# mLSTM stage of a two-block layer on one core: gate rows in four column groups, stabiliser maxima by one fp32r product, denominators as a further value column

## The chip, the cores and the metric

The kernel runs on one core of a Trainium2 chip. The metric is the device time of one execution in microseconds (us); of several runs the median is given. TensorE (PE) has a separate weight loader (PEld); DVE is VectorE, ACT is ScalarE, and SP issues nearly all of the DMAs here.

## The reference, cut to what matters

Two blocks act one after the other on x of 256 tokens by 2048 features, all in float32. The first is attention and a gated feed-forward; the change doesn't touch it. The second has an mLSTM branch with 8 heads (keys of 128, values of 256):

```
proj = h @ w_in + b_in          # q, k, v, o, z_a, i_pre (8), f_pre (8), ...
b = cumsum(log_sigmoid(f_pre)); d_intra = b_l - b_s + i_pre_s   (s <= l)
m_row = max(d_inter, max_s d_intra)            # running stabiliser
scores = (q k^T) * 128**-0.5 * exp(d_intra - m_row)
num = scores @ v;  den = sum_s scores          # (plus the carried state)
h_out = num / max(|den|, exp(-m_row))
h_a = rms_norm(sigmoid(o) * h_out) * silu(z_a);  y_a = h_a @ w_proj_a
```

The kernel computes the mLSTM without chunks: with u = i_pre - b and M = running maximum of u, the weight of key s for query l is exp(-max(M_l - u_s, 0)), masked above the diagonal, and the floor of the denominator is exp(-(b + M)).

## The kernel before

All matrix products with weights go through `step`s. A step is one transfer of 128 x 2048 float32 weights (`raw`), a split into a high part `hi` on ACT (L245) and a low part `lo` on DVE (L246), both in fp32r, and 24 products of 128 x 512 on PE (`group_mm`, L321 to L323: hi by hi, lo by hi, hi by lo), twelve for each half of the tokens (`th`). There are four `raw` buffers and two of `hi` and `lo`. Activations are kept as such pairs too (`khi`, `klo`). `later(n, f)` runs f after the n-th next step; a scheduler then sets the order of each engine's instructions within the data dependences.

The part that the change touches follows the second norm (`barrier2`, where DVE and ACT compute the norm of x and PE has to wait):

- 16 steps of v: the results are evacuated to `V2` (L968), one 128 x 512 tile for each pair of heads and token half.
- One step `if` for the gates: 16 weight columns (8 of i, 8 of f) are padded to 128, loaded as 1 MB, split, and multiplied as 96 fp32r products of 128 x 128 with 128 columns (L983 to L985). `if_rows` then computes log-sigmoid, the cumulated sum b, u (L1015) and M (L1017) on 8 partitions, on ACT and DVE. Three steps later `tr` turns u and exp(-(b+M)) into columns by four small PE transposes (L1024, L1025, `rowT`).
- Then q, k, o and z_a; after every z_a group come two heads (`mlstm`), each in four stages that `later` spreads over the following steps: `qkT` transposes; scores `st` (L1079, L1080) and `mb` (L1082), a float32 product that copies row h of M to all partitions; `den` (L1100 to L1102), three products of the weights `w` with a column of ones, and `num` (L1103 to L1105), three products with v; `hT` transposes.

Of the kernel before, what the change touches and what calls it, by code (L numbers as in the profile page):

```python
# [16 lines left out]
D = 2048  # L17
# [43 lines left out]
K_M0 = 771  # L61
K_M1 = 772
K_SEL = 773
NCONST = 774


def _consts():
    c = np.zeros((128, NCONST), np.float32)
    c[:, K_ID:K_ID + 128] = np.eye(128, dtype=np.float32)
    p = np.arange(128)[:, None]  # L70
    d = 128 + p - np.arange(256)[None, :]
    cnt = ((d >= 0) & (d <= 128)).astype(np.float64)
# [12 lines left out]
    c[:, K_M1] = m1
    c[::32, K_SEL] = 1.0
    return c


def build(tc, A, out):  # L90
# [22 lines left out]
    def ktile32(name="k32"):  # L113
        return kp.tile([128, 512], F32, name=name, tag="k")
# [13 lines left out]
    cols = pp.tile([128, NCOL], F32, name="cols")  # L128
    ident = pp.tile([128, 128], F32, name="ident")
    ones = pp.tile([128, 2], F32, name="ones")  # L130
    ksm = pp.tile([128, NCONST - K_INVA], F32, name="ksm")
    epsc = pp.tile([128, 2], F32, name="epsc")
    x = pp.tile([128, 2, D], F32, name="x")
    cb = pp.tile([128, D], F32, name="cb")
    mod = pp.tile([128, 96], F32, name="mod")
# [21 lines left out]
    def xs_hl(K, k, a, th):  # L157

        e = K[k]
        if isinstance(e, dict):  # L160
            t, c = e[th][a]
            return t[:, c:c + 128]
        return e[:, a, th * 128:(th + 1) * 128]
# [162 lines left out]
        act.activation(dst, ss, AF.Sqrt, bias=epsc[:, 0:1], scale=1.0 / n)  # L326
        dve.reciprocal(dst, dst)

    onesr = pp.tile([128, 128], F32R, name="onesr")
    act.activation(onesr, ones[:, 0:1].to_broadcast([128, 128]), AF.Copy)  # L330

    def row_bcast(c16, g, grow, key):
        hl = sp.tile([128, 2, 4], F32, name="rhl", tag="rhl", bufs=2)
        hr = sp.tile([128, 4], F32R, name="rhr", tag="rhr", bufs=2)
        c = c16[:, 4 * g:4 * g + 4]
        act.activation(hr, c, AF.Copy)
        dve.tensor_copy(hl[:, 0, :], hr.bitcast(F32))
        dve.tensor_sub(hl[:, 1, :], c, hl[:, 0, :])
        d = [kp.tile([128, 512], F32R, name="dg", tag="k") for _ in range(2)]
        for i in range(4):  # L340
            for a in range(2):
                act.activation(d[a][:, i * 128:(i + 1) * 128], ident, AF.Copy, scale=hl[:, a, i:i + 1])
        r = ktile32("rowb")
        if grow is not None:
            nc.sync.dma_start(r, bcast_row(grow[:, 512 * g:512 * g + 512], 512))

        def end():
            p = at_tile("row")
            for a in range(2):
                pe.matmul(p, onesr, d[a], start=(a == 0), stop=(a == 1))  # L350
            if grow is None:
                act.activation(r, p, AF.Copy)
            else:
                dve.tensor_mul(r, r, p)
            GP[key] = r
        later(0, end)
# [6 lines left out]
    nc.sync.dma_start(ksm, A["consts"][:, K_INVA:NCONST])  # L363
# [567 lines left out]
    dn_group(NG - 1)  # L931

    H3 = {}
    mM = pp.tile([128, 128], F32, name="mM")

    def barrier2():
        assert len(gq) <= 16, len(gq)
        nc.sync.dma_start(mM, A["consts"][:, K_MM:K_MM + 128])
        barrier(H3)

    steps[-1] = steps[-1][:5] + (barrier2,)
# [22 lines left out]
                 post=post if kq == 3 else None, fill_n=int(kq in fill))  # L964

    def v2_evac(g, th, p, b):
        V2[g, th] = ktile32("v2")
        dve.tensor_add(V2[g, th], p, b)  # L968

    for g in range(4):  # L970
        tok_steps("v", g, v2_evac)

    R = {}
    uc = pp.tile([128, 32], F32, name="ucols")
# [12 lines left out]

    def if_rows(p):
        rows = []
# [7 lines left out]
        act.activation(g, p[:, :S], AF.Identity, bias=cols[:, C_IF:C_IF + 1])  # L997
# [18 lines left out]
        M = ztile("rowM")  # L1016
# [4 lines left out]
        def tr():  # L1021
# [5 lines left out]
        R["M"] = M  # L1027
        later(3, tr)

    step(A["w_if"], 2048, if_step)  # L1030

    OS = {}
    SZ = {}
# [9 lines left out]
    def za_evac(g, th, p, b):  # L1043
        z = ttile("zb")
        dve.tensor_add(z, p, b)
        SZ[g, th] = ztile("siluz")
# [13 lines left out]
    def mlstm(h, at):  # L1060
# [12 lines left out]
        def s1():  # L1073
            q, k = st["qk"][:, 0:S], st["qk"][:, S:2 * S]
            if h == 0:
                dve.tensor_scalar(hnh, col("headnorm_w_2", 0, 16), 0.5, None, op0=OP.mult)
            M = R["M"]
# [7 lines left out]
            dve.scalar_tensor_tensor(w[:, 0:128], mb[:, 0:128], uc[:, h:h + 1], mM, op0=OP.subtract, op1=OP.max)  # L1085
            dve.tensor_scalar(w[:, 128:256], mb[:, 128:256], uc[:, h:h + 1], 0.0, op0=OP.subtract, op1=OP.max)
            dve.scalar_tensor_tensor(w[:, 256:384], mb[:, 128:256], uc[:, 8 + h:9 + h], mM,
                                     op0=OP.subtract, op1=OP.max)
            act.activation(w, w, AF.Exp, scale=-1.0)
            dve.scalar_tensor_tensor(w, sc[:, 0:384], 128.0 ** -0.5, w, op0=OP.mult, op1=OP.mult)  # L1090
            st["w"] = w

        def s2():
            w = st["w"]
            g, c0 = h // 2, (h % 2) * 256
            v0 = V2[g, 0][:, c0:c0 + 256]
            v1 = V2[g, 1][:, c0:c0 + 256]
            num = at_tile("num")
            dn = at_tile("den")
# [12 lines left out]
            t = ktile32("hn")  # L1112
            jk = ktile32("jk")
            for i in range(2):
                dve.scalar_tensor_tensor(t[:, i * 256:(i + 1) * 256], num[:, i * 256:(i + 1) * 256],
                                         da[:, i:i + 1], OS[g, i][:, c0:c0 + 256], op0=OP.mult, op1=OP.mult)
                act.activation(jk[:, i * 256:(i + 1) * 256], t[:, i * 256:(i + 1) * 256], AF.Square,
                               accum_out=ss[:, i:i + 1])
# [224 lines left out]
def _layout(inp):  # L1343
# [50 lines left out]
    wif = np.zeros((D, 128), np.float32)  # L1394
    wif[:, 0:8] = w[:, 8192:8200]
    wif[:, 32:40] = w[:, 8200:8208]
    a["w_if"] = _blocks(wif)[0]
# [22 lines left out]
```

## Time and profile before

| | |
|---|---|
| three runs | 2477.57, 2478.49, 2479.67 us; median 2478.49 |
| profiled execution | 2476.79 us, of which its span is 2475.0 |
| busy | PE 2410.0 us (97%), weight loads 2023.7 (82%), DVE 1584.8 (64%), ACT 1151.2 (47%) |
| DMA | 597 MB, 241 GB/s on the mean |
| mean granted TensorE clock | 0.991 of full speed |

The span runs from the first to the last instruction; 1.8 us of the execution lie around it. Busy shares are means over stages with different limits, so they say only where to look.

### The profile page before, as it was taken

The page shows a single profiled execution, that of the slowest core. Times are in us where ns is not written, and L with a number is a line of the kernel's source. Part 1 is how long each engine was busy: PE and PEld are TensorE (multiplying, and loading weights), DVE is VectorE, ACT ScalarE, POOL GpSimd, SP SyncE. Part 2 cuts the span into 40 slices and gives each one's busy share as a digit, 9 for nine tenths or more (in the row PEclk, how much of TensorE's full clock was granted, in tenths as well). Part 3 has the DMA queues.
Part 4 walks back from the last instruction along what each step waited for, and adds up shares of the span by engine and source line. Part 5 has one row for each costly group of instructions (what it writes and reads, how often), then busy time and mean ns, then how long its engine had stood idle before and what let it go on. Part 6 is the DMA issues. An engine that isn't in the chain of part 4 may idle for free.

```text
span 2475.0 us, 30384 instructions
## 1 busy us (share of the span) xinstructions
PE 2410.0 (97%) x12508; PEld 2023.7 (82%) x12508; DVE 1584.8 (64%) x1727; ACT 1151.2 (47%) x1415; POOL 0.2 (0%) x4
## 2 busy tenths in 40 slices
PE   6999989999999999999899999999999999999998
PEld 4888988878888888888778888888888888888887
DVE  5888888876666566666664556565456666554555
ACT  5433887653443433334553335455333443444344
POOL 0000000000000000000000000000000000000000
PEclk9999999999999999999999999999999999999999
DMA  8987879847777677677635554555557667555553
GB/s 319 339 332 276 312 280 356 335 187 278 287 266 283 252 282 290 240 298 285 217 115 205 184 191 177 188 178 191 187 211 250 242 249 251 201 198 209 189 193 132
DMA packets 90436, 597.36 MB, mean 241 GB/s; under 512 B 10165, under 2 KB 10805, under 8 KB 20665
## 3 DMA queue, kind: packets, MB, share of 16 engines
q1 hardware_dynamic: 90296, 595.41, 66.1%
q8 instruction: 98, 1.61, 0.3%
q14 instruction: 42, 0.34, 0.0%
HBM read 593.28 MB, written 2.10 MB: 241 GB/s over the span
## 4 chain that ended last, share of the span: by engine, by line
PE 89%; DVE 4%; ACT 3%; DMA 3%; issue 1%; SPq 0%; ACTq 0%; DVEq 0%
PE gu L322 6%; PE gu L321 6%; PE gu L323 6%; PE dn L322 3%; PE dn L323 3%; PE dn L321 3%; PE wo L322 2%; PE wo L321 2%; PE wo L323 2%; PE v L321 2%; PE v L322 2%; PE v L323 2%; DVE lo L246 2%; DMA graw<-i_ada_k 2%; PE z_a L321 1%; PE ga L321 1%
## 5 line engine op out<-in xcount | busy, mean ns | idle before, releaser
L246 DVE TENSOR_TENSOR lo<-raw,hi 128x2048 fp32r<-128x2048 f32 (+3 forms) x446 | 917.1, 2061 | 715.2 <-ACT hi L245 714.9
L245 ACT ACTIVATE hi<-raw 128x2048 fp32r<-128x2048 f32 (+3 forms) x446 | 769.1, 1730 | 1037.2 <-PE gu L323 251.3
L321 PE MATMUL gu<-hi,khi 128*128 128x512 f32 x688 | 268.3, 390 | 0.0
L322 PE MATMUL gu<-lo,khi 128*128 128x512 f32 x688 | 267.8, 389 | 0.0
L323 PE MATMUL gu<-hi,klo 128*128 128x512 f32 x688 | 267.7, 389 | 0.0
L172 DVE SCALAR_TENSOR_TENSOR graw<-graw,cb 128x2048 f32<-128x2048 f32 x112 | 255.9, 2285 | 11.1 <-DMA graw<-i_w_ada 8.7
L322 PEld LDWEIGHTS gu<-lo,khi 128*128 128x128 f32 x688 | 129.2, 188 | 26.8 <-DVE lo L246 0.2
L323 PEld LDWEIGHTS gu<-hi,klo 128*128 128x128 f32 x688 | 129.2, 188 | 26.7
L321 PEld LDWEIGHTS gu<-hi,khi 128*128 128x128 f32 x688 | 129.1, 188 | 26.5
L322 PE MATMUL dn<-lo,khi 128*128 128x512 f32 x336 | 131.0, 390 | 1.5 <-DVE lo L246 1.5
L323 PE MATMUL dn<-hi,klo 128*128 128x512 f32 x336 | 130.8, 389 | 0.0
L321 PE MATMUL dn<-hi,khi 128*128 128x512 f32 x336 | 130.5, 390 | 0.0
L285 PE MATMUL qk<-h,lo 128*128 128x256 f32 x256 | 74.7, 292 | 3.1 <-DVE lo L246 3.1
L283 PE MATMUL qk<-h,hi 128*128 128x256 f32 x256 | 75.7, 296 | 0.1
L322 PEld LDWEIGHTS dn<-lo,khi 128*128 128x128 f32 x336 | 63.1, 188 | 15.2 <-DVE lo L246 2.4
L284 PE MATMUL qk<-h,hi 128*128 128x256 f32 x256 | 74.3, 290 | 0.0
L509 PE MATMUL e<-h,lo 128*128 128x256 f32 x256 | 72.8, 287 | 1.6 <-DVE lo L246 1.6
L323 PEld LDWEIGHTS dn<-hi,klo 128*128 128x128 f32 x336 | 63.1, 188 | 13.2
L321 PEld LDWEIGHTS dn<-hi,khi 128*128 128x128 f32 x336 | 63.1, 188 | 13.1
L507 PE MATMUL e<-h,hi 128*128 128x256 f32 x256 | 73.7, 289 | 0.0
L508 PE MATMUL e<-h,hi 128*128 128x256 f32 x256 | 72.9, 286 | 0.0
L285 PEld LDWEIGHTS qk<-h,lo 128*128 128x128 f32 x256 | 51.0, 199 | 3.5 <-DVE lo L246 3.5
(439 smaller groups left out, 4987.1 us busy)
## 6 DMA issues: line engine op xcount, KB each, us to landing
raw<-i_w_gu SPq DMA_DIRECT2D x88, 1024.0 KB, 4.8
graw<-i_ada_t SPq DMA_DIRECT2D x64, 1024.0 KB, 5.9
graw<-i_w_ada SPq DMA_DIRECT2D x48, 1024.0 KB, 4.8
raw<-i_w_dn SPq DMA_DIRECT2D x44, 1024.0 KB, 4.8
graw<-i_ada_k SPq DMA_DIRECT2D x32, 1024.0 KB, 7.0
raw<-i_w_out SPq DMA_DIRECT2D x32, 1024.0 KB, 5.7
raw<-i_w_s SPq DMA_DIRECT2D x24, 1024.0 KB, 6.8
raw<-i_w_qk SPq DMA_DIRECT2D x16, 1024.0 KB, 7.3
```

The source lines that it names most:

```text
L172: dve.scalar_tensor_tensor(g, g, 1.0, cb, op0=OP.mult, op1=OP.mult, accum_out=dst)
L245: act.activation(hi[:, b:e], r[:, b:e], AF.Copy)
L246: dve.tensor_sub(lo[:, b:e], r[:, b:e], hi[:, b:e].bitcast(F32))
L283: pe.matmul(dst, wh, K[k][:, 0, :], start=s, stop=False)
L284: pe.matmul(dst, wh, K[k][:, 1, :], start=False, stop=False)
L285: pe.matmul(dst, wl, K[k][:, 0, :], start=False, stop=e)
L321: pe.matmul(dsts[th], xh, wh, start=s, stop=False)
L322: pe.matmul(dsts[th], xh, wl, start=False, stop=False)
L323: pe.matmul(dsts[th], xl, wh, start=False, stop=e)
L507: pe.matmul(dst, hv[:, i, c0:c0 + 128], H[k][:, 0, :], start=(k == k0), stop=False)
L508: pe.matmul(dst, hv[:, i, c0:c0 + 128], H[k][:, 1, :], start=False, stop=False)
L509: pe.matmul(dst, lv[:, i, c0:c0 + 128], H[k][:, 0, :], start=False, stop=(k == k1 - 1))
```

## The change

- **Gate rows.** `w_if` is no longer a step. Its 16 columns come as one 128 x 256 tile (`wif`, float32, not split). 64 float32 products have 16 weight columns as the stationary operand and 128 tokens of `khi` or `klo` as the moving one; product k goes to partitions 32*(k mod 4) of the result, so that four accumulations lie in four column groups of the array. ACT copies the four 16-row parts into one tile (`parts`, zeroed on DVE), and two steps later one float32 product with a 0/1 matrix (`ifq`) adds them into the rows that `if_rows` expects.
- **Maxima.** M is split once into an fp32r pair on partitions 0 to 7 and 32 to 39 of `mhl`; `mb` is one fp32r product of 64 rows with a 0/1 selector instead of a float32 product of 8 rows.
- **Denominators.** Each head's values get a 257th column of ones (`V2` tiles of 2 x 272, set by a memset), so `num` yields the denominator too, and the three `den` products go. `num` takes two banks where it took one beside `den`.
- **Buffers.** `V2` moves to the pool `zp`, `siluz` to `kp`, `rowM` to `tp`. The mask `mM` and the selector are loaded at `barrier2` instead of at the start. Small tiles are padded: `x`, `cb`, `mod` move from byte 18432, 34816, 43008 to addresses 64 higher; the pools of large tiles start at multiples of 128 before and after.

```diff
+K_MSEL = 774
+K_IF = 782
+    for h in range(8):
+        c[[h, 32 + h], K_MSEL + h] = 1.0
+    for p in range(128):
+        i = p % 16
+        c[p, K_IF + (i if i < 8 else 24 + i)] = 1.0
...
-    ksm = pp.tile([128, NCONST - K_INVA], F32, name="ksm")
-    epsc = pp.tile([128, 2], F32, name="epsc")
+    ksm = pp.tile([128, K_IF - K_INVA], F32, name="ksm")
+    epsc = pp.tile([128, 16], F32, name="epsc")
...
-                pe.matmul(p, onesr, d[a], start=(a == 0), stop=(a == 1))
+                pe.matmul(p, oner[:, 0:1].to_broadcast([128, 128]), d[a], start=(a == 0), stop=(a == 1))
...
     def barrier2():
-        nc.sync.dma_start(mM, A["consts"][:, K_MM:K_MM + 128])
+        t = ztile("mlc")
+        mlc["hl"] = rtile("mhl")[0:64, 0:S]
+        mlc["M"], mlc["sel"] = t[:, S:S + 128], t[:, S + 128:S + 192]
+        nc.sync.dma_start(mlc["M"], A["consts"][:, K_MM:K_MM + 128])
+        nc.sync.dma_start(mlc["sel"], A["consts"][:, K_IF:K_IF + 64])
+        act.activation(msel, ksm[0:64, K_MSEL - K_INVA:K_MSEL - K_INVA + 8], AF.Copy)
         barrier(H3)
...
     def v2_evac(g, th, p, b):
-        V2[g, th] = ktile32("v2")
-        dve.tensor_add(V2[g, th], p, b)
+        t = zp.tile([128, 2, 272], F32, name="v2", tag="z")
+        dve.memset(t[:, :, 256:257], 1.0)
+        dve.tensor_add(t[:, :, 0:256], p.rearrange("p (a c) -> p a c", a=2), b.rearrange("p (a c) -> p a c", a=2))
+        V2[g, th] = t
...
-    def if_step(hi, lo):
+    def if_load():
+        R["wif"] = ktile32("wif")[:, 0:256]
+        nc.sync.dma_start(R["wif"], A["w_if"])
+    def if_post():
+        wt = R["wif"]
         p = acc_tile("if")
         for th in range(2):
-            dst = p[:, th * 128:(th + 1) * 128]
-            for k in range(KT):
-                wh, wl = hi[:, 128 * k:128 * k + 128], lo[:, 128 * k:128 * k + 128]
-                xh, xl = xs_hl(H3, k, 0, th), xs_hl(H3, k, 1, th)
-                pe.matmul(dst, wh, xh, start=(k == 0), stop=False)
-                pe.matmul(dst, wh, xl, start=False, stop=False)
-                pe.matmul(dst, wl, xh, start=False, stop=(k == KT - 1))
-        if_rows(p)
+            for i in range(4):
+                for a in range(2):
+                    for j in range(4):
+                        k = 4 * i + j
+                        pe.matmul(p[32 * j:32 * j + 16, th * 128:(th + 1) * 128], wt[:, 16 * k:16 * k + 16],
+                                  xs_hl(H3, k, a, th).bitcast(F32), start=(i == 0 and a == 0),
+                                  stop=(i == 3 and a == 1))
+        parts = ttile("ifp")[:, 0:S]
+        dve.memset(parts, 0.0)
+        for j in range(4):
+            act.activation(parts[32 * j:32 * j + 16, :], p[32 * j:32 * j + 16, 0:S], AF.Copy)
+        def end():
+            q = acc_tile("ifq")
+            pe.matmul(q[0:64, 0:S], mlc["sel"], parts, start=True, stop=True)
+            if_rows(q)
+        later(2, end)
...
-    step(A["w_if"], 2048, if_step)
+        hl = mlc["hl"]
+        act.activation(hl, ones[0:64, 0:1].to_broadcast([64, S]), AF.Copy, scale=0.0)
+        act.activation(hl[0:8, :], M[0:8, 0:S], AF.Copy)
+        dve.tensor_sub(hl[32:40, :], M[0:8, 0:S], hl[0:8, :].bitcast(F32))
+    for g in range(4):
+        tok_steps("v", g, v2_evac, post=(None, None, if_load, if_post)[g])
...
-            pe.matmul(mb[:, 0:S], ident[0:8, h:h + 1].to_broadcast([8, 128]), M[0:8, 0:S], start=True,
-                      stop=True)
+            pe.matmul(mb[:, 0:S], msel[:, h:h + 1].to_broadcast([64, 128]), mlc["hl"], start=True, stop=True)
...
-            pe.matmul(dn[:, 0:1], w[:, 0:128], ones[:, 0:1], start=True, stop=True)
-            pe.matmul(dn[:, 1:2], w[:, 128:256], ones[:, 0:1], start=True, stop=False)
-            pe.matmul(dn[:, 1:2], w[:, 256:384], ones[:, 0:1], start=False, stop=True)
-            pe.matmul(num[:, 0:256], w[:, 0:128], v0, start=True, stop=True)
-            pe.matmul(num[:, 256:512], w[:, 128:256], v0, start=True, stop=False)
-            pe.matmul(num[:, 256:512], w[:, 256:384], v1, start=False, stop=True)
+            num = [at_tile("num") for _ in range(2)]
+            pe.matmul(num[0][:, 0:257], w[:, 0:128], v0, start=True, stop=True)
+            pe.matmul(num[1][:, 0:257], w[:, 128:256], v0, start=True, stop=False)
+            pe.matmul(num[1][:, 0:257], w[:, 256:384], v1, start=False, stop=True)
...
-            act.activation(da[:, 0:2], dn[:, 0:2], AF.Abs)
+            for i in range(2):
+                act.activation(da[:, i:i + 1], num[i][:, 256:257], AF.Abs)
```

On PE, where the v steps end and q begins, 96 products stood between them, of which these are the last, with q behind them:

```order
L985 MATMUL if<-khi,lo 128x128
L983 MATMUL if<-khi,hi 128x128
L984 MATMUL if<-klo,hi 128x128
L985 MATMUL if<-khi,lo 128x128
L321 MATMUL q_11026<-hi,khi 128x512
L322 MATMUL q_11026<-lo,khi 128x512
```

Now there are 16 rows of four products, of which these are the last, and `ifq` follows behind the second step of q, with 77 products from there to the first `rowT`:

```order
L1001 MATMUL if<-khi,wif 16x128 x4
L1001 MATMUL if<-klo,wif 16x128 x4
L328 MATMUL q_10981<-hi,khi 128x512
...
L330 MATMUL q_10982<-hi,klo 128x512
L1011 MATMUL ifq<-ifp,mlc 64x256
L328 MATMUL q_10981<-hi,khi 128x512
...
L329 MATMUL k_11141<-lo,khi 128x512
L1051 MATMUL rowT<-ident,rowB 128x8
L330 MATMUL k_11141<-hi,klo 128x512
```

So the gates' products shrink, `ifq` is new, and `rowT` moved from the q steps into the second step of k.

On PE, in head 0, `den` and `num` stood between two steps of o:

```order
L323 MATMUL o_11555<-hi,klo 128x512
L1100 MATMUL den<-ones,w 128x1
L1101 MATMUL den<-ones,w 128x1
L1102 MATMUL den<-ones,w 128x1
L1103 MATMUL num<-v_10502,w 128x256
L1104 MATMUL num<-v_10502,w 128x256
L1105 MATMUL num<-v_10504,w 128x256
L321 MATMUL o_11554<-hi,khi 128x512
```

The same place now:

```order
L330 MATMUL o_11542<-hi,klo 128x512
L1129 MATMUL num<-v_10506,w 128x257
L1130 MATMUL num<-v_10506,w 128x257
L1131 MATMUL num<-v_10509,w 128x257
L328 MATMUL o_11541<-hi,khi 128x512
```

Three products went, and each of the others has one column more. `mb` keeps its place behind `st`.

On DVE, the gate rows' chain (`rowE`, `rowQ`, `rowB`) had its six polynomial steps in one piece, and the evacuations of q (`tq`) stood behind it; now they stand in it:

```order
L1006 TENSOR_SCALAR rowQ<-rowQ 8x256
L246 TENSOR_TENSOR lo<-raw,hi 128x2048
L1008 SCALAR_TENSOR_TENSOR rowQ<-rowQ 8x256 x6
L1009 SCALAR_TENSOR_TENSOR rowQ<-rowQ,rowE 8x256
L1011 SCALAR_TENSOR_TENSOR rowQ<-rowQ,rowE 8x256
L246 TENSOR_TENSOR lo<-raw,hi 128x2048
```

The same stretch of the chain now:

```order
L253 TENSOR_TENSOR lo<-raw,hi 128x2048
L1035 SCALAR_TENSOR_TENSOR rowQ<-rowQ 8x256
L1087 TENSOR_TENSOR tq<-q_10981,bq 128x512
L1035 SCALAR_TENSOR_TENSOR rowQ<-rowQ 8x256
L1087 TENSOR_TENSOR tq<-q_10982,bq 128x512
L1035 SCALAR_TENSOR_TENSOR rowQ<-rowQ 8x256 x3
L253 TENSOR_TENSOR lo<-raw,hi 128x2048
L1035 SCALAR_TENSOR_TENSOR rowQ<-rowQ 8x256
```

The two passes of `lo` stay in the chain, and two evacuations joined it.

## Rows read from the trace of the kernel before

**Rows 1.** The page, part 4: shares of the chain that ended last, by engine.

```profile
PE 89%; DVE 4%; ACT 3%; DMA 3%; issue 1%; SPq 0%; ACTq 0%; DVEq 0%
```

**Rows 2.** Two stretches: busy us of PE, PEld, DVE, ACT, POOL; PEclk, DMA, GB/s.

```profile
1373.00:1395.00 22.00, 21.47 (x96) 17.18 (x96) 18.43 (x24) 9.14 (x9) 0.00 (x0) 1.00 0.47 163
1395.00:1710.00 315.00, 315.00 (x1444) 260.08 (x1443) 179.75 (x212) 151.88 (x158) 0.00 (x0) 1.00 0.52 182
```

**Rows 3.** What PE waited for from 1306 to 2300: total, times, longest.

```profile
PE rowT L1024 <- DVE rowB L1015: 0.5, 1, 0.5
```

**Rows 4.** Timeline of PE where the gate step begins and ends: start, length.

```profile
1360.94 0.22 PE L983 MATMUL if<-khi,hi 128*128 128x128 f32 x1
...
1371.61 0.45 PE L321 MATMUL q<-hi,khi 128*128 128x512 f32 x1
1371.90 0.40 PE L322 MATMUL q<-lo,khi 128*128 128x512 f32 x1
1372.13 0.40 PE L323 MATMUL q<-hi,klo 128*128 128x512 f32 x1
```

**Rows 5.** Timeline of PE around an L194 group, 16 float32 products in column groups.

```profile
300.83 0.28 PE L285 MATMUL qk<-h,lo 128*128 128x256 f32 x1
301.04 1.08 PE L194 MATMUL gv<-graw,cols 128*32 128x128 f32 x32
302.05 0.49 PE L626 MATMUL o<-v,ptS 128*128 128x128 f32 x2
302.38 0.39 PE L627 MATMUL o<-v,ptS 128*128 128x128 f32 x2
```

**Rows 6.** Weight loads of that group, all of L194, and its longest run on PE.

```profile
301.04 0.81 PEld L194 LDWEIGHTS gv<-graw,cols 128*32 128x32 f32 x32
L194 PEld LDWEIGHTS gv<-graw,cols x1024: 105/110/178, 22.6 to 410.9; 128*32 128x32 f32 x171
25.09 2.26 PE L194 MATMUL gv<-graw,cols 128*32 128x128 f32 x54
```

**Rows 7.** Timeline of PE in head 0: den and num between two steps.

```profile
1478.94 0.28 PE L1100 MATMUL den<-ones,w 128*128 128x1 f32 x2
...
1479.52 0.68 PE L1103 MATMUL num<-v,w 128*128 128x256 f32 x2
...
1481.14 0.40 PE L322 MATMUL o<-lo,khi 128*128 128x512 f32 x1
```

**Rows 8.** Timeline of PE in head 1: st and mb before z_a.

```profile
1486.39 0.59 PE L1079 MATMUL st<-mqk 128*128 128x256 f32 x2
1486.82 0.38 PE L1080 MATMUL st<-mqk 128*128 128x128 f32 x2
1487.14 0.69 PE L1082 MATMUL mb<-rowM,ident 8*128 8x256 f32 x2
...
1488.10 0.40 PE L322 MATMUL z_a<-lo,khi 128*128 128x512 f32 x1
```

**Rows 9.** Gate rows: first and last link on ACT and DVE, and q's evacuation.

```profile
1373.52 0.45 ACT L997 ACTIVATE ifs<-if,cols 128x256 f32<-128x256 f32 x1
...
1388.26 0.41 DVE L1015 TENSOR_TENSOR rowB<-ifs,rowB 8x256 f32<-8x256 f32 x1
...
1392.49 0.68 DVE L1055 TENSOR_TENSOR tq<-q,bq 128x512 f32<-128x512 f32 x1
```

**Rows 10.** Head 1: weights ready on DVE, first den on PE.

```profile
1492.15 0.55 DVE L1090 SCALAR_TENSOR_TENSOR w<-st,w 128x384 f32<-128x384 f32 x1
...
1494.00 0.28 PE L1100 MATMUL den<-ones,w 128*128 128x1 f32 x2
```

**Rows 11.** DVE at barrier2: a reciprocal, and the idle time before it.

```profile
1270.77 0.16 DVE L327 RECIPROCAL r<-r 128x1 f32<-128x1 f32 x1 [0.36 <-ACT r L326]
```

**Rows 12.** SP's queue from 1240 to 1420: its longest wait in total.

```profile
SPq L230 <- DVE lo L246: 148.9, 21, 21.4
```

**Rows 13.** The page, part 5: the largest DVE group that reads cb.

```profile
L172 DVE SCALAR_TENSOR_TENSOR graw<-graw,cb 128x2048 f32<-128x2048 f32 x112 | 255.9, 2285 | 11.1 <-DMA graw<-i_w_ada 8.7
```

More of the change, by code (lines that the diff above doesn't have):

```diff
@@ L63 @@
 K_SEL = 773
-NCONST = 774
+K_MSEL = 774
+K_IF = 782
+NCONST = 846
 def _consts():
@@ L327, in rstd_small @@
         dve.reciprocal(dst, dst)
-    onesr = pp.tile([128, 128], F32R, name="onesr")
-    act.activation(onesr, ones[:, 0:1].to_broadcast([128, 128]), AF.Copy)
+    oner = pp.tile([128, 2], F32R, name="oner")
+    act.activation(oner, ones, AF.Copy)
     def row_bcast(c16, g, grow, key):
@@ L362, in build @@
     nc.sync.dma_start(ident, A["consts"][:, K_ID:K_ID + 128])
-    nc.sync.dma_start(ksm, A["consts"][:, K_INVA:NCONST])
+    nc.sync.dma_start(ksm, A["consts"][:, K_INVA:K_IF])
     nc.sync.dma_start(x[:, 0, :], A["x"][:, 0, :])
@@ L933, in build @@
     H3 = {}
-    mM = pp.tile([128, 128], F32, name="mM")
     def barrier2():
         assert len(gq) <= 16, len(gq)
-        nc.sync.dma_start(mM, A["consts"][:, K_MM:K_MM + 128])
+        t = ztile("mlc")
[4 more added lines that the diff above has]
+        act.activation(msel, ksm[0:64, K_MSEL - K_INVA:K_MSEL - K_INVA + 8], AF.Copy)
         barrier(H3)
@@ L966, in v2_evac @@
     def v2_evac(g, th, p, b):
-        V2[g, th] = ktile32("v2")
-        dve.tensor_add(V2[g, th], p, b)
-    for g in range(4):
-        tok_steps("v", g, v2_evac)
+        t = zp.tile([128, 2, 272], F32, name="v2", tag="z")
+        dve.memset(t[:, :, 256:257], 1.0)
+        dve.tensor_add(t[:, :, 0:256], p.rearrange("p (a c) -> p a c", a=2), b.rearrange("p (a c) -> p a c", a=2))
+        V2[g, th] = t
     R = {}
+    msel = pp.tile([64, 8], F32R, name="msel")
+    mlc = {}
     uc = pp.tile([128, 32], F32, name="ucols")
-    def if_step(hi, lo):
+    def if_load():
[3 more added lines that the diff above has]
+        wt = R["wif"]
         p = acc_tile("if")
         for th in range(2):
-            dst = p[:, th * 128:(th + 1) * 128]
-            for k in range(KT):
-                wh, wl = hi[:, 128 * k:128 * k + 128], lo[:, 128 * k:128 * k + 128]
-                xh, xl = xs_hl(H3, k, 0, th), xs_hl(H3, k, 1, th)
-                pe.matmul(dst, wh, xh, start=(k == 0), stop=False)
-                pe.matmul(dst, wh, xl, start=False, stop=False)
-                pe.matmul(dst, wl, xh, start=False, stop=(k == KT - 1))
-        if_rows(p)
+            for i in range(4):
[14 more added lines that the diff above has]
+        later(2, end)
     def if_rows(p):
@@ L996, in if_rows @@
         g = ttile("ifs")[:, :S]
-        act.activation(g, p[:, :S], AF.Identity, bias=cols[:, C_IF:C_IF + 1])
+        act.activation(g[0:64, :], p[0:64, :S], AF.Identity, bias=cols[0:64, C_IF:C_IF + 1])
         f = g[32:40, :]
@@ L1015, in if_rows @@
         dve.tensor_sub(u, g[0:8, :], b)
-        M = ztile("rowM")
+        M = ttile("rowM")
         dve.tensor_tensor_scan(M[0:8, 0:S], u, u, 0.0, op0=OP.max, op1=OP.bypass)
@@ L1026, in tr @@
             dve.tensor_copy(uc, pt[:, 0:32])
-        R["M"] = M
         later(3, tr)
-    step(A["w_if"], 2048, if_step)
+        hl = mlc["hl"]
[4 more added lines that the diff above has]
+        tok_steps("v", g, v2_evac, post=(None, None, if_load, if_post)[g])
     OS = {}
@@ L1045, in za_evac @@
         dve.tensor_add(z, p, b)
-        SZ[g, th] = ztile("siluz")
+        SZ[g, th] = ktile32("siluz")
         act.activation(SZ[g, th], z, AF.Tanh, scale=0.5)
@@ L1076, in s1 @@
                 dve.tensor_scalar(hnh, col("headnorm_w_2", 0, 16), 0.5, None, op0=OP.mult)
-            M = R["M"]
             sc = at_tile("st")
@@ L1081, in s1 @@
             mb = at_tile("mb")
-            pe.matmul(mb[:, 0:S], ident[0:8, h:h + 1].to_broadcast([8, 128]), M[0:8, 0:S], start=True,
-                      stop=True)
+            pe.matmul(mb[:, 0:S], msel[:, h:h + 1].to_broadcast([64, 128]), mlc["hl"], start=True, stop=True)
             w = ttile("w")[:, 0:384]
-            dve.scalar_tensor_tensor(w[:, 0:128], mb[:, 0:128], uc[:, h:h + 1], mM, op0=OP.subtract, op1=OP.max)
+            dve.scalar_tensor_tensor(w[:, 0:128], mb[:, 0:128], uc[:, h:h + 1], mlc["M"], op0=OP.subtract, op1=OP.max)
             dve.tensor_scalar(w[:, 128:256], mb[:, 128:256], uc[:, h:h + 1], 0.0, op0=OP.subtract, op1=OP.max)
-            dve.scalar_tensor_tensor(w[:, 256:384], mb[:, 128:256], uc[:, 8 + h:9 + h], mM,
+            dve.scalar_tensor_tensor(w[:, 256:384], mb[:, 128:256], uc[:, 8 + h:9 + h], mlc["M"],
                                      op0=OP.subtract, op1=OP.max)
@@ L1095, in s2 @@
             g, c0 = h // 2, (h % 2) * 256
[L1096 to L1099, printed above, removed]
-            pe.matmul(dn[:, 0:1], w[:, 0:128], ones[:, 0:1], start=True, stop=True)
-            pe.matmul(dn[:, 1:2], w[:, 128:256], ones[:, 0:1], start=True, stop=False)
-            pe.matmul(dn[:, 1:2], w[:, 256:384], ones[:, 0:1], start=False, stop=True)
-            pe.matmul(num[:, 0:256], w[:, 0:128], v0, start=True, stop=True)
-            pe.matmul(num[:, 256:512], w[:, 128:256], v0, start=True, stop=False)
-            pe.matmul(num[:, 256:512], w[:, 256:384], v1, start=False, stop=True)
+            v0 = V2[g, 0][:, h % 2, 0:257]
+            v1 = V2[g, 1][:, h % 2, 0:257]
+            num = [at_tile("num") for _ in range(2)]
+            pe.matmul(num[0][:, 0:257], w[:, 0:128], v0, start=True, stop=True)
+            pe.matmul(num[1][:, 0:257], w[:, 128:256], v0, start=True, stop=False)
+            pe.matmul(num[1][:, 0:257], w[:, 256:384], v1, start=False, stop=True)
             da = small("da")
-            act.activation(da[:, 0:2], dn[:, 0:2], AF.Abs)
+            for i in range(2):
+                act.activation(da[:, i:i + 1], num[i][:, 256:257], AF.Abs)
             ss = small("mss")
@@ L1114, in s2 @@
             for i in range(2):
-                dve.scalar_tensor_tensor(t[:, i * 256:(i + 1) * 256], num[:, i * 256:(i + 1) * 256],
+                dve.scalar_tensor_tensor(t[:, i * 256:(i + 1) * 256], num[i][:, 0:256],
                                          da[:, i:i + 1], OS[g, i][:, c0:c0 + 256], op0=OP.mult, op1=OP.mult)
@@ L1393, in _layout @@
         a["w_" + name + "2"] = _groups(w[:, o:o + n])
[L1394 to L1397, printed above, removed]
+    a["w_if"] = np.ascontiguousarray(w[:, 8192:8208].reshape(KT, 128, 16).transpose(1, 0, 2)).reshape(128, 256)
     a["w_pa"] = _groups(g["w_proj_a_2"][0])
```

## Prediction

> **What bounds the kernel now.** I read the chain that ended last first [rows 1]: 89% of it is PE, and no other engine holds more than 4%. A share of the whole says little of one stage, so next come the windows. Over the 315 us in which the heads run between weight steps, PE is busy in all 315.00, DVE in 180 and ACT in 152, at a granted clock of 1.00 and a DMA share of 0.52 [rows 2]. The list of PE's waits from 1306 to 2300 holds one wait of work that the change touches, `rowT` for `rowB`, once, 0.5 us [rows 3]. So in this stage time that leaves PE leaves the kernel, time that leaves DVE, ACT or the DMA queues is worth nothing, and a new wait of PE counts in full. That fixes the method: I price PE's products by the distance from one start to the next in the timeline (lengths overlap, since products are pipelined), and then ask whether their inputs still come in time.
>
> The cadence is .23 us per product of 128 x 512 (1371.90 to 1372.13 of [rows 4]), about 5.5 us for a step of 24. Where a block ends with such a step, I take one cadence from the start of the step's second product.
>
> **Gate rows.** The old block runs from 1360.94 to 1371.90 - .23 = 1371.67: 10.73 us for 96 products, .112 each [rows 4]. The new one has 64 float32 products with 16 stationary columns and 128 moving ones, in four column groups. The kernel has such products already: a `gv` group of 16 takes 301.04 to 302.05 = 1.01 us [rows 5], .063 each, with the change to and from narrow tiles in it. Its weight loads take .81 us for 32 passes [rows 6], .025 a pass, so I put the stream at .027 a pass and the way in and out at some .36: 128 x .027 + .36 = 3.8 us. By .063 it would be 4.0. The longest run of `gv` is dearer, 2.26 us for 27 products, .084 each, or 5.4 us for 64 [rows 6]; it stands at the start of the kernel, where PE waits for data. Bounds 3.6 and 5.4, value 3.8, nearest to the group that has PE to itself: **saves 6.95 us** (5.3 to 7.1).
>
> `ifq` is new: a float32 product of 256 columns takes .43 us (`st`, 1486.39 to 1486.82, [rows 8]), and I add .2 for the change of tile: **costs .6** (.4 to .8).
>
> The rule that speaks against this part: the Trainium skill, "TensorE: Matmul & The Clock Gate", section "The mechanism" (Part 3), says that a weight load overlaps products in flight only when its row group differs. All four column groups here use all 128 rows, so by it no load would be hidden. The trace disagrees for the same shape: .81 us of loads lie within 1.01 us in which the products run too [rows 5, 6]. By the rule the block would take 27.8 us instead of 3.8 (the second rival has the working).
>
> **Denominators.** In head 0 `den` and `num` take 1478.94 to 1481.14 - .23 = 1480.91, 1.97 us [rows 7]. The 256-column float32 price of .43 [rows 8] makes the three `num` 1.29; the 257th column is 1/256 of that, .005. What is left, .68, is `den` with its loads, and it goes in all 8 heads: **saves 5.4 us**. The start of `num` in the trace stands only .58 behind `den` (1479.52), which gives 4.6; bounds 4.4 and 5.5.
>
> **Maxima.** In head 1 `mb` holds PE from 1487.14 to 1488.10 - .23 = 1487.87, .73 us [rows 8]. Of it .43 is the price of 256 float32 columns; about .30 is the change to an 8-row tile and back. An fp32r product streams 256 columns in half the .23 of 512, .11. Nothing in the trace shows an fp32r product of 64 rows. If the .30 stays, it costs .41 and saves .32; if nothing is gained, 0; if the .30 goes too and only the .11 is left, .62 a head. I take .32, since 64 rows are still a part of the array: 8 x .32, **saves 2.6 us** (0 to 5.0).
>
> **Waits: what is late next.** (a) The gates' chain. It runs from `ifs` at 1373.52 to the last `rowB` at 1388.67, 15.1 us, on ACT and DVE in turn [rows 9], and PE waited .5 us at its end [rows 3]. Now it starts behind `ifq`, two steps of q later, and `rowT` follows `ifq` by 77 products, 17.6 us. Two evacuations of q of .68 each [rows 9] join the chain on DVE; the rest is unchanged. 15.1 + 1.4, plus up to 1.5 when an ACT pass over `hi` stands ahead of it, is 16.5 to 18: a wait of 0 to .5 us, as before. Behind `rowT` on PE stand the rest of that k step and all that follows. (b) The weights `w` of the odd heads. DVE ends them at 1492.70 and PE takes them at 1494.00, 1.30 us of slack [rows 10]. PE now comes some .6 + .3 us earlier, so .4 is left; DVE's and ACT's work ahead of `w` is not shorter. (c) `da` now waits for `num` rather than `den`, under 1 us later, but what PE wants of it (`hT`) comes a step, 5.5 us, behind. I allow **.5 us** for all of this together; its upper bound, 1 us in each of the four odd heads and 2 at `rowT`, is a rival.
>
> **At no cost.** The `if` step's 1 MB load, its `hi` and its `lo` go; DVE and ACT are idle half the time there, so that is no gain either. Eight memsets on DVE stand at barrier2, where DVE idles .36 us for ACT [rows 11]; uncovered they would cost PE about .1 us each, since PE waits for that norm. The loads of mask, selector and biases move to other places in SP's queue, which waits 148.9 us for `lo` in that stretch [rows 12]: SP is ahead of its buffers, and uncovered each is one small issue. The copies of `parts`, and M's pair, run on ACT and DVE beside PE. `onesr` becomes a broadcast, with the same products. `v0`'s order on PE shifts by some 8 products, whose pairs come just in time: +-.5 us, value 0. The shift of `x`, `cb` and `mod` by 64 bytes has no row that prices it. L172 reads `cb` 112 times at 2285 ns, 255.9 us in all [rows 13], and beside it nothing reads these tiles as often. I take 0; the far end is a rival.
>
> **The sum.** 6.95 - .6 + 5.4 + 2.6 - .5 = **13.9 us**. The profiled execution took 2476.79 us (its span of 2475.0 and 1.8 around it) and becomes 2462.9. It lies 1.7 below the median of the runs, so on their scale 2478.5 - 13.9 = **2464.6 us**. All terms at their good ends (7.1 - .4 + 5.5 + 5.0) save 17.2, to 2461.3; all at their bad ends (5.3 - .8 + 4.4 + 0 - 1) save 7.9, to 2470.6.
>
> **Rivals.**
> 1. *The column groups don't run beside each other* when every product has its own weights: 64 x 2 passes x .107 (a quarter of `st`'s .43) = 13.7 us, 3 more than before, and the sum falls to 13.9 - 9.9 = 4.0: 2474.5 us, within 0.2%. Against it: 16 such products took 1.01 us and not 3.4 [rows 5]. Chance .04.
> 2. *No weight load is hidden*, each product waiting for its own: 128 x (.110 for a load, the mean of L194's in [rows 6], + .107) = 27.8 us. The gate block grows by 17.1, and the change ends at 2478.5 + 17.1 - 6.9 (the other terms as above) = **2488.7 us**: slower. It decides once the block takes over 17.6 us, .138 a pass; [rows 5] show .032. This is what the rule cited at the gate rows would do here. Chance .03.
> 3. *The shifted addresses slow DVE.* The 112 passes of L172 would have to grow by .17 us, 7%, to eat the gain and 5 us more, and all of that would have to lie on the path, where DVE holds 4% [rows 1]. With 7%, 2478.5 + 5 = 2483.5 us. Nothing in the rows speaks for it but that the addresses move. Chance .02.
> 4. *New waits of PE*: the .4 of slack in the odd heads is used up and each waits 1 us, and `rowT` 2: 13.9 + .5 - 6 = 8.4 saved, 2470 us. For it: the slack is the smallest number in the sum. Chance .15.
> 5. *`mb` gains nothing*, since the change of tile sets its price: 11.3 saved, 2467 us, inside the forecast's own range. Chance .25.
>
> **How the numbers follow.** The forecast with its small variants (rival 5 among them) holds .74: 2461.3 to 2470.6, and I move the lower end to 2460 for the spread of a run (2 us between the three). Rival 4 lies at that range's upper edge; to hold a part of it, the range reaches to 2471. The other three, and mishaps that I don't see (.02), .11 together, stay outside. 0.2%, or 5 us, is about what a measurement of this kernel can tell from no change. Faster by more than that: forecast and rival 4, .89; within: rival 1 and the unseen, .06; slower: rivals 2 and 3, .05.
>
> **What would show it.** The gate block on PE: 3.6 to 4.0 us from its first product to q's; over 10 refutes the gate term. `ifq` .6. `num` starts right behind the product of o, three times .43, with no gap in front. `mb` about .4 to the next product's start; .7 refutes it, .2 means that the half-height tile is free. Among PE's waits, `rowT` under 1 us and `w` in the odd heads near nothing; a row of `num` waiting for `w` with a total of some us is rival 4. L172's mean stays at 2.29 us. PE's idle time at barrier2 stays. The forecast would be wrong if time that PE gives back were met by a late weight load or a late `lo`: then PE's waits from 1306 on would show those names where now they show none.

## The result and the profile after

| | median, us | runs | ratio to before, 95% interval |
|---|---|---|---|
| before | 2478.03 | 2477.03 to 2479.67 | |
| changed | 2510.10 | 2508.43 to 2511.08 | 1.0126 [1.0112, 1.0140] |

The change made the kernel slower by 32 us (medians of four runs each), where 13.9 us faster was forecast. The places that the change touches behave nearly as forecast, and their rows come first. Timeline of PE in the changed kernel (start, length), at the gate step, `ifq`, `st` with `mb`, and `num`; they answer to [rows 4, 7, 8]:

```profile
1382.97 0.40 PE L330 MATMUL v<-hi,klo 128*128 128x512 f32 x1
1383.30 0.41 PE L1001 MATMUL if<-khi,wif 128*16 128x128 f32 x8
...
1386.92 0.50 PE L328 MATMUL q<-hi,khi 128*128 128x512 f32 x1
1387.25 0.39 PE L329 MATMUL q<-lo,khi 128*128 128x512 f32 x1
...
1397.98 0.40 PE L330 MATMUL q<-hi,klo 128*128 128x512 f32 x1
1398.31 0.65 PE L1011 MATMUL ifq<-ifp,mlc 128*64 128x256 f32 x2
1398.88 0.50 PE L328 MATMUL q<-hi,khi 128*128 128x512 f32 x1
1399.22 0.39 PE L329 MATMUL q<-lo,khi 128*128 128x512 f32 x1
...
1490.33 0.38 PE L1113 MATMUL mb<-mhl,msel 64*128 64x256 f32 x1
1490.65 0.33 PE L1101 MATMUL qkT<-ident,tq 128*128 128x128 f32 x1
...
1496.49 0.40 PE L330 MATMUL o<-hi,klo 128*128 128x512 f32 x1
1496.72 0.59 PE L1129 MATMUL num<-v,w 128*128 128x257 f32 x2
1497.15 0.60 PE L1130 MATMUL num<-v,w 128*128 128x257 f32 x2
1497.59 0.60 PE L1131 MATMUL num<-v,w 128*128 128x257 f32 x2
1497.83 0.58 PE L328 MATMUL o<-hi,khi 128*128 128x512 f32 x1
1498.26 0.39 PE L329 MATMUL o<-lo,khi 128*128 128x512 f32 x1
```

The gate block lasts from 1383.30 to 1387.25 - .23 = 1387.02, 3.72 us; `num` stands right behind o and follows itself by .43. PE's list of waits from 1306 to 2300, where `rowT` stood before [rows 3], is empty now. The loss must lie elsewhere. The page, first part, of the changed kernel (us busy, share, instructions):

```profile
span 2507.3 us, 30366 instructions
PE 2442.6 (97%) x12486; PEld 2013.4 (80%) x12486; DVE 1584.3 (63%) x1736; ACT 1151.8 (46%) x1429; POOL 0.2 (0%) x4
```

PE is busy 32.6 us longer than before (2410.0) with 22 instructions less, and the span grew by 32.3. So PE did not come to wait: its products take longer. A stretch in the gated feed-forward of the first block, which the change doesn't touch (columns as in [rows 2]), first before, then after:

```profile
800.00:1200.00 400.00, 399.32 (x1782) 330.86 (x1781) 254.39 (x174) 157.51 (x117) 0.00 (x0) 1.00 0.74 272
```

```profile
800.00:1200.00 400.00, 399.88 (x1747) 324.59 (x1746) 249.51 (x172) 156.35 (x117) 0.00 (x0) 1.00 0.73 267
```

PE is full in both at a granted clock of 1.00, and ends 35 products fewer in the same time. The starts say how: in the changed kernel,

```profile
899.99 0.40 PE L329 MATMUL gu<-lo,khi 128*128 128x512 f32 x1
900.23 0.40 PE L330 MATMUL gu<-hi,klo 128*128 128x512 f32 x1
900.47 0.40 PE L328 MATMUL gu<-hi,khi 128*128 128x512 f32 x1
900.70 0.39 PE L329 MATMUL gu<-lo,khi 128*128 128x512 f32 x1
900.93 0.39 PE L330 MATMUL gu<-hi,klo 128*128 128x512 f32 x1
901.16 0.39 PE L328 MATMUL gu<-hi,khi 128*128 128x512 f32 x1
```

the steps are .24, .24, .23, .23, .23. Over all pairs of 128 x 512 products that follow each other without a pause (some 8740 pairs) the mean distance of two starts, called the cadence here, is 227.0 ns before and 232.5 after. Before, 94% of them stand at 226 or 227; after, they run through short cycles, 229, 238 in some stretches and 229, 230, 232, 241, 233, 231, 231 in others. There are 8960 such products: 8960 x 5.5 = 49 us lost. Those of 256 columns became a little faster, 118.7 instead of 119.8 ns, 1.7 us in the 1536 that use `hi` or `lo`. So 32 us is what is left of a loss of some 47 and a gain of some 14.

What differs for a product that the change doesn't touch is where its operands lie. The tiles' byte addresses in a partition:

| | khi, klo (stationary) from | hi, lo (moving) | hi - khi, rest by 256 |
|---|---|---|---|
| before | 45184 | 194688, 211072 | 0 |
| changed | 44288 | 194944, 211328 | 128 |

`khi` and `klo` come in buffers of 2048 bytes and are read at multiples of 512, `hi` and `lo` at multiples of 2048, so one rest holds for all products of a step. It moved because the `z` pool lies between them: its nine buffers grew from 2048 to 2176 bytes with the tiles of `v2`, 1152 bytes in all, 128 more than a multiple of 256. The small tiles ahead of the `k` pool shrank by 896, which moves both sides alike.

### The profile page after: what moved, and what is told of

It reads as the page before. It is cut to its first block, busy times and chain, and to the rows that moved or that the text cites. A ratio compares the mean times of both kernels' runs of the same rounds, so it can differ in the third digit from the quotient of the medians.

```text
span 2507.3 us, 30366 instructions
## 1 busy us (share of the span) xinstructions
PE 2442.6 (97%) x12486; PEld 2013.4 (80%) x12486; DVE 1584.3 (63%) x1736; ACT 1151.8 (46%) x1429; POOL 0.2 (0%) x4
## 4 chain that ended last, share of the span: by engine, by line
PE 91%; ACT 3%; DVE 3%; DMA 2%; issue 1%; SPq 0%; ACTq 0%; DVEq 0%
PE gu L328 6%; PE gu L330 6%; PE gu L329 6%; PE dn L329 3%; PE dn L330 3%; PE dn L328 3%; PE wo L328 2%; PE wo L329 2%; PE wo L330 2%; PE v L328 2%; PE v L329 2%; PE v L330 2%; PE z_a L328 1%; PE ga L328 1%; PE zb L330 1%; PE bg L330 1%
## 5 line engine op out<-in xcount | busy, mean ns | idle before, releaser
L329 PE MATMUL v<-lo,h 128*128 128x512 f32 x128 | 52.6, 411 | 1.5 <-DVE lo L253 1.5
```

The lines of the kernel that those rows point to most:

```text
L329: pe.matmul(dsts[th], xh, wl, start=False, stop=False)
```

## The experiments

Theory D: the distance between the addresses of the two operands sets the cadence. Rivals: A, each operand's own address counts; N, the addresses don't matter, and something else that is new does it. Four kernels, two of them the kernel before with nothing but unused bytes, and a memset of one element of them, added.

**a_gap**, the changed kernel:

```diff
+    gapp = ctx.enter_context(tc.tile_pool(name="gapp", bufs=1))
+    gap = gapp.tile([128, 96], F32, name="gap")
     tp = ctx.enter_context(tc.tile_pool(name="tp", bufs=TBUFS))
...
+    dve.memset(gap[:, 0:1], 0.0)
```

> The changed kernel with 384 unused bytes between the pools of z and t, so that hi and lo (moving operand) move from 194944 and 211328 to 195328 and 211712 while khi and klo (stationary operand) stay at 44288 and up: the distance of the two becomes a multiple of 512 bytes, as it was before the change. Theory D (the distance of the two operands' addresses sets the cadence of the 128 x 512 products): the cadence returns from a mean of 232 to 227 ns, 8960 products give back 8960 x 5.5 ns = 49 us, and the time falls to about 2461. Theory A (an operand's own address counts, khi's or hi's): hi changes, khi doesn't, so 2461 if hi alone decides and 2510 if khi does. Theory N (not addresses, but something else in the change): 2510.

**a_shift**, the changed kernel:

```diff
     epsc = pp.tile([128, 16], F32, name="epsc")
+    gap = pp.tile([128, 96], F32, name="gap")
     x = pp.tile([128, 2, D], F32, name="x")
...
+    dve.memset(gap[:, 0:1], 0.0)
```

> The changed kernel with the same 384 bytes ahead of x, so that all large tiles move together: khi to 44672 (128 modulo 512, as before the change), hi to 195328. The distance stays as in the changed kernel. Theory D: cadence 232 ns, about 2510 us. Theory A: about 2461 where khi's own address decides. Theory N: 2510.

**b_gap** and **b_shift**, the kernel before with the same two edits and 32 elements in place of 96:

> The kernel before with nothing but 128 unused bytes between the pools of z and t: hi and lo move from 194688 and 211072 to 194816 and 211200, khi and klo stay. Distance of the operands 128 modulo 512 instead of 0. Theory D: cadence 232 instead of 227 ns, about 2478 + 45 to 49 = 2525 us. Theory A: the same only where hi's own address decides. Theory N: 2478.

> The kernel before with 128 unused bytes ahead of x: khi moves from 45184 to 45312 and hi from 194688 to 194816, together. The distance stays a multiple of 512. Theory D: no change, 2478 us. Theory A: 2525 us or so, since both operands' own addresses change. Theory N: 2478.

| | hi - khi, rest by 256 | median, us | ratio to before | cadence 512, ns |
|---|---|---|---|---|
| a_gap | 0 | 2465.21 | 0.9942 [0.9927, 0.9956] | 226.9 |
| a_shift | 128 | 2511.32 | 1.0125 [1.0110, 1.0140] | 232.7 |
| b_gap | 128 | 2524.64 | 1.0176 [1.0159, 1.0193] | 232.6 |
| b_shift | 0 | 2478.35 | 0.9994 [0.9985, 1.0004] | 227.0 |

The time follows the distance in both kernels and the common shift in neither. `hi` starts at the same 194816 in b_gap and b_shift and is slow in one and fast in the other, and `khi` stays where it was in b_gap, so A is out; b_gap holds nothing else of the change, so N is out. a_gap stands 4 us over the 2461 expected: the 49 us left out that the products of 256 columns lose their 1.7 us again, and the other 2 are within the spread of the runs. The same stretch in a_gap, and in b_gap, where not one instruction of the kernel before was changed but a memset added:

```profile
800.00:1200.00 400.00, 399.30 (x1783) 330.84 (x1782) 255.41 (x176) 158.74 (x117) 0.00 (x0) 1.00 0.75 274
```

```profile
800.00:1200.00 400.00, 400.00 (x1745) 324.20 (x1745) 248.98 (x172) 156.40 (x117) 0.00 (x0) 1.00 0.74 267
```

1783 and 1745 products: before and after again. The effect is worth 2524.64 - 2479.66 = 45.0 us in the one kernel (before took 2479.66 beside these runs) and 2510.10 - 2465.21 = 44.9 in the other (46.1 by a_shift, which ran beside a_gap).

**Which part of the change carries it.** The changed kernel with `den` and `num` as before and v2 tiles of 2 x 256:

```diff
-        t = zp.tile([128, 2, 272], F32, name="v2", tag="z")
-        dve.memset(t[:, :, 256:257], 1.0)
+        t = zp.tile([128, 2, 256], F32, name="v2", tag="z")
...
-            pe.matmul(num[0][:, 0:257], w[:, 0:128], v0, start=True, stop=True)
+            pe.matmul(dn[:, 0:1], w[:, 0:128], ones[:, 0:1], start=True, stop=True)
...
```

> The changed kernel without its value column: v2 tiles of 2 x 256 again, den and num as before the change; gate rows, maxima, moved tiles and the 64 bytes of x, cb and mod stay as changed. Without the 128 bytes that each of the nine z buffers had grown by, hi lies at 193792 and khi at 44288, a multiple of 256 apart. Theory D: cadence 227 ns, so the time of a_gap plus the den term of 5.4 us, about 2470.6. Rival: the loss is carried by another part (the shift of x, cb and mod): then the cadence stays at 232 and the time is about 2515 us.

> a_gap a second time, beside a_noden on the same chip, for the size of the den term: 2465 us, 5.4 us under a_noden.

a_noden took 2470.23 us, 0.9967 [0.9956, 0.9978] of before, at the fast cadence (227.0 ns); a_gap_again 2465.06, 0.9952 [0.9940, 0.9965]. The stretch of the feed-forward in a_noden:

```profile
800.00:1200.00 400.00, 399.43 (x1782) 330.90 (x1782) 253.73 (x174) 158.72 (x116) 0.00 (x0) 1.00 0.74 272
```

So the value column, which saves some 5 us of work, is what cost 45 by the size of its tile; the 64 bytes by which `x`, `cb` and `mod` are still moved in a_noden cost nothing that shows. The 5.2 us between the two medians agree with the `den` term, but their intervals overlap, so these runs don't size it by themselves.

**The distance by itself.** A kernel of products alone, each line another distance:

```diff
+    st = pp.tile([128, 512], F32R, name="st")
+    mv = pp.tile([128, 4096], F32R, name="mv")
...
+    for (s, m), e0, e1 in seq(96, 512): pe.matmul(p[:, 0:512], st[:, s:s + 128], mv[:, m + 32:m + 32 + 512], start=e0, stop=e1)  # 512 at 128
```

> A kernel of products alone: all of the reference's work is left out, and the output is a copy of x. fp32r products of 128 x 512, in the order of a step (two stationary tiles 1024 bytes apart, two moving ones 8192 apart), 96 in a row for each distance between moving and stationary operand, from 0 to 2048 bytes, then the same with 256 columns from 0 to 512. Theory D: 227 ns at distances of 0 and multiples of 512 bytes, 232 at 128, and a fixed value at each distance between; for 256 columns 120 at 0 and 119 at 128. Rival: the cadence differs only while DVE, ACT or the DMA engines read and write the same memory; here they rest, and then all distances show one cadence.

Groups by line of that run (busy us, mean ns): 512 columns at 0, 64, 128 and 256 bytes, then 256 columns at 0, 128 and 192:

```profile
L119 PE MATMUL acc<-mv,st 128*128 128x512 f32 x96 | 21.9, 389 | 0.0
L129 PE MATMUL acc<-mv,st 128*128 128x512 f32 x96 | 22.1, 391 | 0.0
L133 PE MATMUL acc<-mv,st 128*128 128x512 f32 x96 | 22.6, 395 | 0.0
L141 PE MATMUL acc<-mv,st 128*128 128x512 f32 x96 | 21.9, 389 | 0.0
L173 PE MATMUL acc<-mv,st 128*128 128x256 f32 x96 | 11.7, 283 | 0.0
L181 PE MATMUL acc<-mv,st 128*128 128x256 f32 x96 | 11.6, 281 | 0.0
L185 PE MATMUL acc<-mv,st 128*128 128x256 f32 x96 | 11.1, 276 | 0.0
```

From start to start, in ns (one run; means of each line without its first steps):

| bytes | 0 | 4 | 16 | 32 | 64 | 96 | 128 | 160 | 192 | 224 | 256 |
|---|---|---|---|---|---|---|---|---|---|---|---|
| 512 columns | 226.7 | 236.7 | 231.7 | 233.3 | 228.9 | 233.3 | 233.4 | 234.3 | 233.4 | 233.4 | 226.7 |
| 256 columns | 120.0 | | | 117.8 | 117.8 | 120.0 | 118.7 | 117.3 | 113.3 | 118.3 | 120.0 |

From 256 on the row repeats, as far as it was run (to 2048 for 512 columns, 512 for 256). A last line at 0 gives 226.7 again, so nothing drifted. The rival of this run falls: DVE, ACT and DMAs rest, and the values are close to those of the kernels (at 0 and 128: 226.7 and 233.4 here, 227.0 and 232.5 there). Two kernels carry the table back:

**a_gap128** and **a_gap192**: as a_gap, with 32 and 48 elements.

> The changed kernel with 128 unused bytes between the pools of z and t, where a_gap had 384: distance between hi and khi 256 modulo 512. By the run of products alone the pattern repeats every 256 bytes, so 227 ns and 2465 us, as a_gap. If the rest of a multiple of 512 counts: 232 ns and 2510 us.

> The same with 192 unused bytes: distance 64 modulo 256 for the products of 512 columns, whose moving operand is hi or lo, and 192 for those of 256 columns in the first block, where hi and lo are stationary. By the run of products alone: 228.9 ns instead of 226.7 for 8960 products, +20 us, and 113.3 instead of 120 for some 1600, -10 us; in sum 2475 us against the 2465 of a_gap. If other engines' reads and writes shift the pattern, the cadences differ from these two values.

a_gap128 took 2466.40 us, 0.9948 [0.9932, 0.9965], at 227.0 ns: the period is 256 bytes in the kernel too. a_gap192 took 2480.32, 1.0004 [0.9995, 1.0013], 5 us over what was expected. The direction of both cadences is right, 229.3 and 114.5 ns, but each is a little worse than alone (228.9, 113.3). By the measured ones, 8960 x 2.33 (229.28 - 226.95) = +20.9 and 1536 x 5.3 (119.8 - 114.5) = -8.1, or +12.8 against a_gap; its PE is indeed busy 12.9 us longer (2407.9 against 2395.0). It took 15.1 us more than a_gap and 13.9 more than a_gap128, which ran beside it; the 1 to 2 us that are left are within the spread of the runs.

**Both distances at their best.**

```diff
-            hi = hp.tile([128, 2048], F32R, name="hi", tag="hi")
+            o = 16 * any(n in steps[i][2].__qualname__ for n in (".e_step.", ".qk_step."))
+            hi = hp.tile([128, 2112], F32R, name="hi", tag="hi")[:, o:o + 2048]
...
```

(and `lo` likewise; the unused bytes of the pool are 224, which makes the rest of hi - khi 0.)

> The changed kernel with both distances at their best: gap so that hi and khi lie a multiple of 256 apart for the products of 512 columns, and in the steps of the attention's e and qk, where hi is stationary and h moves 256 columns, hi and lo start 64 bytes later in their buffers (8448 bytes long). To make room the tiles of v2 are 2 x 260 instead of 2 x 272. By the run of products alone 1536 products take 113.3 instead of 120 ns: 10 us less, 2455 us, if PE bounds the attention. Rival: the attention's steps wait for weight loads (DMA share .9 there), and what PE saves is waited for: 2465 us.

It took 2458.03 us, 0.9914 [0.9899, 0.9928] of before: faster than both kernels, 7 us under a_gap and 8.4 under a_gap128, which ran beside it. The products of 256 columns stand 114.9 ns apart instead of 119.8, which is 7.5 us in 1536, and PE is busy 8.1 us less than in a_gap (2386.9 against 2395.0). So what PE saves in the attention arrives, as far as the spread of the runs can tell, and the rival, that it would be waited for, falls. The 10 us expected took the 113.3 of the run alone.

**Which reads meet.** Products alone once more, with two stationary tiles in turn:

```diff
+    for (s, m), e0, e1 in run(512, 288, 0, 2080, n=96): pe.matmul(p[:, 0:512], st[:, s:s + 128], mv[:, m:m + 512], start=e0, stop=e1)  # 512 own 0, other 128
```

> Products alone again (all of the reference's work is left out). Two products take turns, with stationary tiles s0 and s1. In one set each moving operand lies at a multiple of 256 bytes from its own stationary operand and at 32 to 192 bytes from the one that is loaded next; in the second set it is the other way round; in the third both distances are the same. Theory L (the stream of a moving operand and the load of the next weights read the memory at once, and their distance counts): the second set is fast, 226.7 ns, and the first as slow as the third at 128 (233). Theory O (a product's own pair counts): first set fast, second slow. Besides, 128 and 384 columns and float32 products at 0, 64, 128 and 192 bytes, for which no theory says anything yet: if the load of 128 columns alone decided, the extra time at 128 bytes would be the same some 7 ns for all lengths.

In the table, own is the distance to a product's own stationary operand, other the one to the stationary operand that is loaded next, and the columns name bytes.

| ns from start to start, 512 columns | 32 | 64 | 128 | 192 |
|---|---|---|---|---|
| own distance 0, other as above | 231.7 | 231.8 | 236.7 | 231.5 |
| own as above, other 0 | 230.0 | 231.6 | 230.0 | 233.3 |
| both as above | 233.4 | 228.9 | 232.4 | 233.3 |

In the first two rows the two products that take turns have opposite distances: where one has 64, the next has 256 - 64 = 192. Only the column of 128 has one distance. Its first two rows, as groups:

```profile
L131 PE MATMUL acc<-mv,st 128*128 128x512 f32 x96 | 22.9, 397 | 0.0
L133 PE MATMUL acc<-mv,st 128*128 128x512 f32 x96 | 22.2, 392 | 0.0
```

Neither theory holds: nothing but both at 0 gives 226.7 (the first line of the run), and at 128 the own distance costs less than the other. Both enter, and not as a sum. Nor do the two distances fix the value: in the second row the columns 64 and 192 have the same two, with the products' parts swapped, and take 231.6 and 233.3. The order of the products counts as well: 256 columns with both distances at 192 take 117.8 here, where the order of the run before gave 113.3.

Other lengths: 384 columns take 173.3 at 0 and 176.0 at 128; 128 columns 111.6 to 111.7 at all four distances, so the extra at 128 is not one constant. A float32 product stands as two records in the trace, called passes in the prediction; from one to the next it is 429.2 ns (512 columns) and 215.8 (256) at every distance tried, so a product takes twice that. The rows at 0 and 128 (48 products each):

```profile
L197 PE MATMUL acc<-x 128*128 128x512 f32 x96 | 41.4, 592 | 0.0
...
L203 PE MATMUL acc<-x 128*128 128x512 f32 x96 | 41.4, 592 | 0.0
```

That two reads of PE meet in the memory is thus only argued. Shown is that the cadence of fp32r products of 512 columns depends on the distance with the other engines at rest, with a period of 256 bytes, and that of the distances tried only multiples of 256 give 226.7 ns. What else sets the value away from 0 stays open.

## Why the prediction was wrong, step by step

**The step that failed** is in the part at no cost, where moved addresses were priced: "The shift of `x`, `cb` and `mod` by 64 bytes has no row that prices it ... I take 0". It asked which tiles the change moves on purpose and who reads them, and left out those that moved because a pool below them grew: `hi` and `lo` against `khi` and `klo`. With that the method's own base, .23 us a product in [rows 4] before and after, was wrong: each of 8960 products takes 2.4% longer, 49 us by the starts and 45 us of the kernel's time. The cadence was not among the signs of being wrong that the prediction named. Rival 3 suspected addresses, but those of the wrong tiles and on the wrong engine: it put them on DVE, whose reader of `cb` takes as long as before. This row answers to [rows 13]:

```profile
L179 DVE SCALAR_TENSOR_TENSOR graw<-graw,cb 128x2048 f32<-128x2048 f32 x112 | 255.9, 2285 | 9.3 <-DMA graw<-i_w_ada 7.9 <-DMA graw<-i_ada_t 1.3
```

No row of the trace before could price the distance, since its weight products of 512 columns all stood at one. That the distance changed could be read from the pools; they were looked at as far as multiples of 128, which hold before and after, and the period is 256.

**The other steps** can be weighed in a_gap, where only that term is taken out: 2465.21 us, 14.5 under the before of its runs, for a forecast of 13.9.

- Gate rows: forecast 3.8 us, 3.72 in the changed kernel, with .33 instead of .23 ahead of it: the saving is 6.9. That 3.8 came so near is partly luck: its .36 for the way in and out followed from no row, since 32 passes of .027 leave .15 of the 1.01 us in [rows 5], which makes 3.6. The column groups run beside each other as the `gv` rows said, and rival 1 is out. Rival 2 too: a load takes 97 ns (the row below). Even if the four groups load side by side, one group's 32 loads make 3.1 us and its 32 passes at rival 1's .107 another 3.4, and the whole block took 3.72, so loads and passes overlap. The Trainium skill says in "TensorE: Matmul & The Clock Gate", section "The mechanism", that a weight load overlaps products in flight only when its row group differs, where the same section, some lines before, also names the background weight buffer as a way to go ahead. These loads all use 128 rows, so for them the first statement doesn't hold; no run here tells whether the second is what happened.

```profile
L1001 PEld LDWEIGHTS if<-khi,wif x64: 92/97/97, 1383.3 to 1386.4; 128*16 128x16 f32 x64
```

- `ifq`: from 1398.31 to 1399.22 - .23, .68 us, and with the .33 instead of .23 ahead of it (1397.98 to 1398.31) .78: .2 more than forecast.
- `den`: 1496.72 to 1498.26 - .23 = 1.31 us for `num` alone; .66 saved a head, 5.3 in all, forecast 5.4.
- `mb`: in a_gap, head 1, from 1482.06 to 1482.70 - .23, .41 us instead of .73, as forecast: the .30 around it stays, and rival 5 is out.

```profile
1482.06 0.38 PE L1116 MATMUL mb<-mhl,msel 64*128 64x256 f32 x1
1482.37 0.50 PE L331 MATMUL z_a<-hi,khi 128*128 128x512 f32 x1
1482.70 0.39 PE L332 MATMUL z_a<-lo,khi 128*128 128x512 f32 x1
```

- Waits: at the fast cadence `rowT` waits .2 us where it waited .5, and `num` doesn't stand among PE's waits at all, so the .5 allowed wasn't needed, and rival 4 is out. The row of a_gap that answers to [rows 3]:

```profile
PE rowT L1054 <- DVE rowB L1045: 0.2, 1, 0.2
```

6.9 - .8 + 5.3 + 2.6 + .3 = 14.3, against 14.5 measured. By its interval the 14.5 are 10.9 to 18.1, and the other runs of the changed kernel with that distance, a_gap_again and a_gap128, give 13.5 and 13.3. So these terms hold; that they meet the measurement to .2 us is more than the runs can tell.

## What to carry to other kernels

When a change resizes a buffer, list the addresses of the operands of the products that it doesn't touch, and their distances before and after; a tile that grows moves every pool above it. In an fp32r stream whose weights change with each product, keep the distance of moving and stationary operand at a multiple of 256 bytes for 512 columns, or try a few paddings: they cost a few hundred bytes and were worth 45 us here, three times the work saved. For 256 columns 192 over a multiple was best in this kernel's order of products (114.9 ns against 119.8) but not in another order, so there the padding has to be tried in the kernel itself. When a kernel slows and PE stays full, compare the number of products in equal windows of a stage that wasn't changed before looking for waits.

## What the runs showed that was not expected

Products whose instructions the change left alone took 2.4% longer, in a stretch where PE is full in both kernels at a granted clock of 1.00. At one and the same distance the changed kernel goes through two different cycles of steps. And float32 products don't depend on the distance at all: 429.2 ns a pass of 512 columns at each one tried.

Every operand here starts at a multiple of its element size, which is what the Trainium skill asks in "SBUF — State Buffer", section "Operand start alignment"; that section speaks of what is legal, not of time. In "TensorE: Matmul & The Clock Gate", section "Step-by-step: what each phase is for", the Trainium skill says that the stream and the weight load have independent read ports and that loading the next weights takes no bandwidth from the running product. By that one would expect no distance to matter; 226.7 against 233.4 ns at 128 bytes, and 236.7 at 4, with all other engines at rest, show that for fp32r it does. Whether the two reads themselves get in each other's way, no run here shows. For float32 no run here contradicts the page of the Trainium skill.
